# The first phase of a hybrid attention and convolution layer, rebuilt: latent tokens in two halves, adaLN in blocks of 256 channels by matmuls in four column strips

## The chip, the cores and the metric

One core of one Trainium2 chip runs the whole layer in one launch. The metric is the device time in microseconds (us), the median of the runs shown. The engines are named as in the profile: PE is the matrix engine (PEld its weight loads), DVE the vector engine, ACT the scalar engine, POOL the GpSimd engine. SP issues most of the DMAs. L12 is line 12 of the kernel. Lines of the kernel before are meant unless "of the changed kernel" stands beside them.

## The reference, cut to what matters

There are 1024 latent tokens and 256 context tokens of 1024 channels. All are normalised, scaled and shifted (adaLN), and go through one projection to 3840 columns that feeds three branches. The first phase of the kernel computes `h`.

```python
# D_MODEL = 1024, SEQ = 1024, CTX_LEN = 256, DEPTH = 1, all float32
def rmsnorm(x, g):
    y = x * lax.rsqrt(jnp.mean(x * x, axis=-1, keepdims=True) + NORM_EPS)
    return y * g
# per layer; the context goes through the same weights with c_ctx in place of c
shift, scale, gate = split3(silu(c) @ w_ada + b_ada)      # w_ada (1024, 3072)
h = rmsnorm(x, norm_g) * (1 + scale) + shift
z = h @ w_in                                              # w_in (1024, 3840)
# z: 4 x 256 columns short convolution, 4 x 512 attention (q, k, v, gate), 3 x 256 conformer
y = concat(short_conv_branch(...), neighbourhood_attention(...) * silu(gate), conformer_branch(...))
x = x + gate * (y @ w_out)
```

The attention's queries see a window of the latent grid, with a bias by relative position from a learned table, and all context keys.

## The kernel before

**Numbers in two parts.** For its large products PE takes each float32 array as a high and a low part (`hi`, `lo`), and three products replace one: high by high, high by low, low by high (`mm_k`, L374 to L376). So h is kept as `h0` (high) and `h1` (low), its context part as `hc0`, `hc1`, and the projection weights `wr` are split into `wh` by ACT (L128) and `wl` by POOL (L129).

**The first phase** is the function `start`. A string of tokens, `SEQ`, sets the order in which it emits its work, and on PE, DVE, ACT and POOL the work stays in that order. The DMAs all go through SP, one in-order queue, and eight semaphores in turn tell of their end, so each DMA there also waits for the one eight before it. The letters: `X` loads 128 tokens, `q` squares and sums them, `r` takes the inverse root, `x` scales them (L997). `L` loads adaLN weights. `a`, `b`, `c` transpose one block of 128 channels of the first latent half, the second latent half, or the context, so that channels lie on the partitions (`h_trans`, L327). `f`, `g`, `h` apply scale and shift and make the high part (`h_mod`); `u`, `v`, `o` make the low part (L351). `m`, `n` project a block of the first or second half onto the first pair's queries and keys. `Q` writes these to their tiles (queries L403, keys L422); `Q00` is followed by the scaling of the bias table `sg` (L498).

**adaLN** there is made per 128 channels, from rows of 512 bytes (L211), in three ways: blocks 0 and 6 by matmuls of split weights, blocks 1, 2 and 4 by float32 matmuls of two columns (`ada_mm32`, L241), blocks 3, 5 and 7 by products on DVE (`ada_acc`, L252 and L254), which small matmuls by ones then sum (L262). In h_mod, ACT (L342) or DVE (L340) writes the modulated block `h_raw` from PSUM, ACT copies its high part (L347), and DVE or POOL subtracts (L351).

**After the phase** PE's order is still the order of the code; the other engines and SP follow a scheduler's list. PE projects the context keys of the first pair (`proj_pair`), then the conformer's first two projections (`cf_in`: two of them, each over two latent halves, 24 matmuls per half), then the values (`v_proj`, L462). Beside that the bias tables are made: `sg` goes to the DRAM tables `dpr`, `dpm` (L503 to L509), from these to seven tables `u` (L517), from these to the tables `bt` of the first two heads (L533). The adaLN gate (`ada_gates`) loads 16 pieces `t` of weights (L840), and DVE sums them (L843, L845). The weights of the values are loaded at L448.

Of the kernel before, what the change touches and what calls it, by code (L numbers as in the profile page):

```python
# [52 lines left out]
g00 W00 C1 D301 b1 B2 g10 W10 v00 b3 w00 R2 b2 X1 v11 C2 w10 L40 X2 X0 X3 E3 n0 g21 g31 q10 v21 v31 q01 n1 n2 q20 L41  # L53
r02 L61 q30 L60 x11 r21 s61 x01 n3 s60 x21 L51 r31 x31 B4 a0 f01 t610 R4 a2 f21 u00 a1 t601 a3 W11 A6 D511 u20 f10 W01
m0 a4 u10 L50 C4 w01 f30 X9 b4 D501 m1 w11 f40 R6 L71 X8 u40 L70 u31 m2 C6 g40 a5 v40 q80 a6 E5 m3 q90 D701 f50 f60 n4
b6 D711 m4 b5 r82 u50 m5 g60 g50 v51 a7 b7 E7 x80 O x91 u60 f70 v60 g71 m6 n5 c0 u71 c1 h00 h11 m7 c3 c2 o01 Q00 n6
v70 o11 h20 n7 h31 o21 o31 Q02 Q01 Q10 Q12 Q11
# [3 lines left out]
def f32(ap):  # L61
    return ap.bitcast(F32)


class Builder:
# [14 lines left out]
    # ---- order of emission: TensorE work is traced in the order in which it shall run; coroutines  # L80
    # yield how far TensorE shall get before they go on ----
# [58 lines left out]
    def columns(self, name, rows):  # L140
        # rows of 128 channels, turned into one column per row
# [12 lines left out]
    def constants(self, crows):  # L154
# [8 lines left out]
        self.ones = cp.tile([P, 1], F32, name="ones")  # L163
        nc.gpsimd.memset(self.ones, 1.0)
# [6 lines left out]
        self.stat = stat = cp.tile([P, KT, 2, 2], F32R, name="stat")  # L171
        thv = th.rearrange("p (s k) -> p k s", s=2)
        self.stat32 = cp.tile([P, KT, 2], F32, name="stat32")
        nc.scalar.activation(out=self.stat32, in_=thv, func=AF.Copy, scale=0.5)
        nc.scalar.activation(out=stat[:, :, :, 0], in_=thv, func=AF.Copy, scale=0.5)
        self.stat_done = nc.vector.scalar_tensor_tensor(out=stat[:, :, :, 1], in0=thv, scalar=0.5, in1=f32(stat[:, :, :, 0]),
                                       op0=ALU.mult, op1=ALU.subtract)
# [28 lines left out]
    def ada_load(self, k, g):  # L206
        hk = KT // 2
        wa = self.sp_w.tile([P, hk, 2, P], F32, name="wa", bufs=7)
        for s in range(2):
            src = self.a["w_ada"][g * hk * P:(g + 1) * hk * P, s * D + k * P:s * D + (k + 1) * P]  # L210
# [3 lines left out]
    def ada_hi(self, w):  # L214
        hk = KT // 2
        wh = self.sp_w.tile([P, hk, 2 * P], F32R, name="wah", bufs=3)
        self.nc.scalar.activation(out=wh, in_=w, func=AF.Copy)
        return w, wh

    def ada_lo(self, w, wh, eng):  # L220
        wl = self.sp_w.tile([P, KT // 2, 2 * P], F32R, name="wal", bufs=3)
        eng.tensor_tensor(out=wl, in0=w, in1=f32(wh), op=ALU.subtract)
        return wh, wl

    def ada_mm(self, parts):
        nc = self.nc
        hk = KT // 2
        pa = self.ps_a.tile([P, HALF], F32, name="ps_a")
        for j in range(2):
            for kk in range(KT):  # L230
                st = self.stat[:, kk].rearrange("p s h -> p (s h)")
                nc.tensor.matmul(pa[0:4, 0:2 * P], lhsT=st, rhs=parts[kk // hk][j][:, kk % hk],
                                 start=(j + kk == 0), stop=(j == 1 and kk == KT - 1))
        return pa

    def ada_mm32(self, parts):
        nc = self.nc
        hk = KT // 2
        pa = self.ps_a.tile([P, HALF], F32, name="ps_a")
        for kk in range(KT):  # L240
            nc.tensor.matmul(pa[0:2, 0:2 * P], lhsT=self.stat32[:, kk], rhs=parts[kk // hk][:, kk % hk],  # L241
                             start=(kk == 0), stop=(kk == KT - 1))
        return pa

    def ada_acc(self, w, acc, g, first, eng):
        # half of the sum over 1024 rows for both conditioning vectors, still spread over the partitions
        hk = KT // 2
        for i in range(hk):
            for v in range(2):
                c, a = self.stat32[:, g * hk + i, v:v + 1], acc[:, v]  # L250
                if first and i == 0:
                    eng.tensor_scalar(out=a, in0=w[:, i], scalar1=c, scalar2=None, op0=ALU.mult)  # L252
                else:
                    eng.scalar_tensor_tensor(out=a, in0=w[:, i], scalar=c, in1=a, op0=ALU.mult, op1=ALU.add)  # L254

    def ada_sum(self, k, acc):
        nc = self.nc
        pa = self.ps_a.tile([P, HALF], F32, name="ps_a")
        for s in range(2):
            for v in range(2):  # L260
                c = 2 * s + v
                nc.tensor.matmul(pa[:, c:c + 1], lhsT=acc[:, v, s * P:(s + 1) * P], rhs=self.ones, start=True, stop=True)  # L262
        self.ada_mod(k, pa[:, 0:4].rearrange("p (s c) -> p s c", s=2))

    def ada_row(self, pa, n):
        row = self.sp_s.tile([4, 2 * P], F32, name="ada_row", bufs=1)[0:n]
        self.nc.scalar.activation(out=row, in_=pa[0:n, 0:2 * P], func=AF.Copy)
        return pa, row

    def ada_cols(self, k, pa, row):  # L270
        nc = self.nc
        n = row.shape[0]
        pt = pa[:, 2 * P:2 * P + 2 * n]
        for s in range(2):
# [958 lines left out]
```

## Time and profile before

| what | value |
|---|---|
| median of 3 runs (lowest to highest) | 637.64 us (636.84 to 638.3) |
| profiled execution, its span | 639.5 us |
| PE busy | 600.4 us, 94% of the span |
| DVE, ACT, POOL busy | 423.3, 258.0, 205.8 us |
| first phase on PE ends | 83.3 us |
| values' projection starts on PE | 109.70 us |
| granted PE clock 29.9 to 59.0 us, 59.0 to 83.3 us | 0.88, 0.86 |

The profiled execution has no time of its own but its span, 1.86 us above the median of the runs. The rows of the profile give the start in us, the duration, engine, line, operation, output and inputs, shapes and count; in brackets, how long the engine was idle before and what released it. A float32 matmul leaves two records. SPq is SP's queue as it issues DMAs.

### The profile page before, as it was taken

Reading aid. Unit: us, or ns where it says so; the run is one execution under the profiler, and the core shown is the slowest. Engines: PE = TensorE matmul, PEld = TensorE weight load, DVE = VectorE, ACT = ScalarE, POOL = GpSimd, SP = SyncE. Lnnn points to the kernel's source line nnn. Section 1 sums busy time; section 2 is a strip of 40 time slices with the busy share of each in tenths; the row PEclk is TensorE's granted clock in tenths of the full one; section 3 lists DMA queues with packets and bytes.
Section 4 is the critical chain, followed back from the end, with each engine's and each line's share of the span. In section 5 each row is a group of like instructions: output and inputs, shape, how many; then the busy total and the mean of one; then the engine's idle time right before and its main releaser. Section 6 shows DMA issues by size and latency. Waiting matters only on the chain.

```text
span 639.5 us, 9011 instructions
## 1 busy us (share of the span) xinstructions
PE 600.4 (94%) x3089; PEld 500.5 (78%) x3089; DVE 423.3 (66%) x709; ACT 258.0 (40%) x488; POOL 205.8 (32%) x213
## 2 busy tenths in 40 slices
PE   3888799969999999999999999999999999999995
PEld 1456678847889888888888888888887888888885
DVE  2889795848935669957889666773789726353343
ACT  4565571111125543344542455523645434331222
POOL 2467720021024322233331334232333261066112
PEclk9987899998999999999999999999999999999998
DMA  8991189454672303632116334145221165671122
GB/s 273 327 311 47 24 240 154 135 142 132 181 188 69 68 24 86 176 90 60 47 46 176 81 71 97 46 123 150 51 51 34 46 200 172 212 273 52 67 99 99
DMA packets 105619, 78.65 MB, mean 123 GB/s; under 512 B 26763, under 2 KB 89317, under 8 KB 105445
## 3 DMA queue, kind: packets, MB, share of 16 engines
q1 hardware_dynamic: 103845, 71.51, 41.2%
q10 hardware_dynamic: 1728, 6.55, 3.0%
q8 instruction: 25, 0.41, 0.3%
q14 instruction: 21, 0.17, 0.1%
HBM read 55.93 MB, written 14.29 MB: 110 GB/s over the span
## 4 chain that ended last, share of the span: by engine, by line
PE 73%; DVE 9%; SPq 5%; DMA 5%; issue 3%; POOL 2%; ACT 2%; POOLq 0%; DVEq 0%; ACTq 0%
PE ps_z L375 13%; PE ps_z L376 13%; PE ps_z L374 13%; PE po L651 5%; PE ps_t L639 5%; PE ps_f L898 5%; PE ps_f L900 5%; PE ps_f L899 5%; PE ps_s L620 3%; PE ps_s L621 2%; DVE acc L254 2%; PE ps_z L462 2%; SPq L211 2%; PE ps_z L464 2%; PE ps_z L463 2%
## 5 line engine op out<-in xcount | busy, mean ns | idle before, releaser
L374 PE MATMUL ps_z<-h,wh 128*128 128x512 f32 x408 | 162.0, 397 | 1.5 <-DVE kt L422 1.5
L375 PE MATMUL ps_z<-h,wh 128*128 128x512 f32 x408 | 160.8, 394 | 1.2 <-POOL h L351 1.2
L376 PE MATMUL ps_z<-h,wl 128*128 128x512 f32 x408 | 160.7, 394 | 0.0
L129 POOL TENSOR_TENSOR wl<-wr,wh 128x512 fp32r<-128x512 f32 x52 | 71.3, 1374 | 138.9 <-ACT wh L128 121.5
L630 POOL TENSOR_SCALAR pr<-pr,sm 128x640 f32<-128x640 f32 (+1 forms) x64 | 53.0, 828 | 138.5 <-DVE sm L629 122.7
L376 PEld LDWEIGHTS ps_z<-h,wl 128*128 128x128 f32 x408 | 77.3, 189 | 16.9
L374 PEld LDWEIGHTS ps_z<-h,wh 128*128 128x128 f32 x408 | 77.5, 190 | 14.9 <-issue 1.7
L375 PEld LDWEIGHTS ps_z<-h,wh 128*128 128x128 f32 x408 | 77.4, 190 | 14.6 <-POOL h L351 1.5
L716 DVE SCALAR_TENSOR_TENSOR acc<-t,half_w,acc 128x1024 f32<-128x1024 f32 x60 | 82.9, 1381 | 1.1
L643 ACT ACTIVATE pw<-ps_t 128x640 fp32r<-128x640 f32 (+1 forms) x64 | 43.5, 679 | 90.8 <-PE ps_t L639 90.8
L625 DVE CUSTOM_DVE_ANT_0 ps_s<-ps_s,bt 128x640 f32<-128x640 f32 (+1 forms) x64 | 50.9, 796 | 33.7 <-PE ps_s L621 31.9
L644 DVE TENSOR_TENSOR pw<-ps_t,pw 128x640 fp32r<-128x640 f32 (+1 forms) x64 | 50.4, 788 | 17.2 <-ACT pw L643 16.9
L628 ACT ACTIVATE pr<-ps_s,mn 128x640 f32<-128x640 f32 (+1 forms) x64 | 49.1, 766 | 20.0 <-DVE mn L625 19.2
L651 PE MATMUL po<-pw,vt 128*128 128x256 f32 x304 | 51.4, 298 | 2.1 <-DVE yb L602 1.2
L898 PE MATMUL ps_f<-woh,y 128*128 128x512 f32 (+1 forms) x136 | 51.6, 380 | 0.0
L900 PE MATMUL ps_f<-woh,y 128*128 128x512 f32 (+1 forms) x136 | 51.6, 379 | 0.0
L899 PE MATMUL ps_f<-wol,y 128*128 128x512 f32 (+1 forms) x136 | 51.6, 379 | 0.0
L128 ACT ACTIVATE wh<-wr 128x512 fp32r<-128x512 f32 x52 | 32.7, 628 | 38.3 <-PE ps_z L375 18.0
L639 PE MATMUL ps_t<-ident,pr 128*128 128x128 f32 x304 | 43.6, 272 | 0.0
L651 PEld LDWEIGHTS po<-pw,vt 128*128 128x128 f32 x304 | 40.4, 190 | 3.9 <-issue 3.5
L620 PE MATMUL ps_s<-kt,qd 128*128 128x384 f32 (+1 forms) x128 | 42.2, 350 | 0.5 <-ACT pr L628 0.4
L639 PEld LDWEIGHTS ps_t<-ident,pr 128*128 128x128 f32 x304 | 36.0, 142 | 1.7 <-issue 0.9
(174 smaller groups left out, 938.6 us busy)
## 6 DMA issues: line engine op xcount, KB each, us to landing
wr<-in_w_in SPq DMA_DIRECT2D x52, 256.0 KB
wa<-in_w_ada SPq DMA_DIRECT2D x32, 256.0 KB
qd<-qn SPq DMA_DIRECT2D x32, 256.0 KB
vd<-t SPq DMA_DIRECT2D x20, 256.0 KB
x_in<-in_x SPq DMA_DIRECT2D x8, 512.0 KB
t<-in_w_ada SPq DMA_DIRECT2D x16, 256.0 KB
vt<-vd SPq DMA_DIRECT2D x32, 128.0 KB
fraw<-in_w_out SPq DMA_DIRECT2D x8, 512.0 KB
```

What stands on the lines that cost most here:

```text
L129: i2 = (eng or nc.vector).tensor_tensor(out=lo, in0=src, in1=f32(hi), op=ALU.subtract)
L374: nc.tensor.matmul(ps, lhsT=wh, rhs=hh, start=(k == 0), stop=False)
L375: nc.tensor.matmul(ps, lhsT=wh, rhs=hl, start=False, stop=False)
L376: self.last = nc.tensor.matmul(ps, lhsT=wl, rhs=hh, start=False, stop=(k == KT - 1))
L620: nc.tensor.matmul(win, lhsT=q[:, b % 4], rhs=kwin, start=(i == 0), stop=(i == 1))
L630: nc.gpsimd.tensor_scalar(out=pr, in0=pr, scalar1=sm, scalar2=0.5, op0=ALU.mult, op1=ALU.mult)
L639: nc.tensor.transpose(out=pt[:, c * P:(c + 1) * P], in_=pr[:, c * P:(c + 1) * P], identity=self.ident)
L651: self.nc.tensor.matmul(po, lhsT=vt[:, vi, h], rhs=pw[:, c], start=(c == 0), stop=(c == n - 1))
L716: self.after_pe(nc.vector.scalar_tensor_tensor(out=acc, in0=u[:, t:t + T], scalar=self.half_w[:, 2 * t + ct:2 * t + ct + 1], in1=acc, op0= ...
L898: nc.tensor.matmul(ps, lhsT=yh, rhs=wh[:, ch], start=(first and i == 0), stop=False)
L899: nc.tensor.matmul(ps, lhsT=yh, rhs=wl[:, ch], start=False, stop=False)
L900: nc.tensor.matmul(ps, lhsT=yl, rhs=wh[:, ch], start=False, stop=(last and i == len(chs) - 1))
```

## The change

The first phase is rewritten; nothing behind the first context keys is, but for one swap on PE.

- The latent tokens go in two halves. Tokens 0 to 511 (`X0` to `X3`) are loaded first, and all of adaLN and of their projection (`a`, `f`, `u`, `m`) is done before tokens 512 to 1023 are squared and scaled; then come their `b`, `g`, `v`, `n`, then the context. Loads `X4` to `X9` stand last in the phase.
- adaLN is made per 256 channels in one way. `B(k, g)` issues four float32 matmuls, whose stationary operand is 32 columns (the two conditioning vectors, the rest zeros) and which stream 512 columns into the 32-partition strip i of one PSUM bank. `R` copies the bank to SBUF on ACT, `C` sums the strips by four small float32 matmuls with `sel` (ones where the strips have the two vectors), and three small DVE operations follow. The splits, the products on DVE and their sums by ones are gone.
- Its weights come in 16 loads of 512 KB in rows of 1 KB, where there were 32 loads of 256 KB.
- h_mod makes the high part on ACT straight from PSUM and the raw block on DVE, also from PSUM; the low part is always DVE's. All `x` scalings are on DVE.
- After the phase PE takes the first half of the first conformer projection ahead of the context keys.

```diff
 SEQ = """
-s00 X5 L10 K s01 t001 t010 A0 X7 X4 X6 L11 L31 q50 R0 q41 L20 C0 q70 L30 r42 x51 B1 q60 x41 r62 L21 D311 x70 x60 b0 R1
...
-v70 o11 h20 n7 h31 o21 o31 Q02 Q01 Q10 Q12 Q11
+X0 X1 L00 X2 X3 L01 K W00 W10 L10 L11 L20 L21 W01 W11 L30 L31 X4 X5 X6 X7 X8 X9
+q00 q11 r02 x01 x11 B00 q20 q31 r22 x21 x31 a0 a1 B01 R0 w00 w10 C0
+f0 u0 f1 u1
+B10 m0 B11 R1 m1 a2 C1 a3 f2 u2 f3 u3
+B20 m2 B21 R2 m3 w01 w11 a4 C2 a5 f4 u4 f5 u5
+B30 m4 B31 R3 q40 m5 q51 a6 C3 a7 f6 r42 u6 f7 u7 x41 x51 q60 q71 r62 x61 x71
+m6 m7 b0 b1 g0 v0 g1 v1 b2 O Q00
+n0 b3 g2 v2 n1 b4 g3 v3 n2 b5 g4 v4 n3 b6 g5 v5 n4 b7 g6 v6 q80 q91 n5 g7 v7 Q01 r82 n6 x81 x91 n7
+c0 Q02 c1 h0 o0 h1 o1 c2 c3 h2 o2 h3 o3 Q10 Q11 Q12
 """
...
     def ada_load(self, k, g):
         hk = KT // 2
-        wa = self.sp_w.tile([P, hk, 2, P], F32, name="wa", bufs=7)
+        wa = self.sp_w.tile([P, hk, 2, 2 * P], F32, name="wa", bufs=5)
...
+    def ada_mm(self, pa, w, g):
+
         hk = KT // 2
         for i in range(hk):
+            self.nc.tensor.matmul(pa[32 * i:32 * i + 32], lhsT=self.stat[:, g * hk + i], rhs=w[:, i],
+                                  start=(g == 0), stop=(g == 1))
+
+    def ada_row(self, pa):
+        row = self.sp_s.tile([P, HALF], F32, name="ada_row", bufs=1)
+        self.nc.scalar.activation(out=row, in_=pa, func=AF.Copy)
+        return row
 
     def ada_cols(self, k, pa, row):
         nc = self.nc
+        for i in range(4):
+            nc.tensor.matmul(pa[:, 2 * i:2 * i + 2], lhsT=row[:, i * P:(i + 1) * P], rhs=self.sel, start=True, stop=True)
...
+    def h_mod(self, ps, k, t0, src):
...
+        for i in range(1 + src):
+            scl, shift = self.scl[:, k + i, src:src + 1], self.shift[:, k + i, src:src + 1]
+            sl = slice(i * n, (i + 1) * n)
+            nc.scalar.activation(out=hi[:, sl], in_=ps[:, sl], func=AF.Identity, scale=scl, bias=shift)
+            nc.vector.tensor_scalar(out=raw[:, sl], in0=ps[:, sl], scalar1=scl, scalar2=shift, op0=ALU.mult, op1=ALU.add)
         return lo, raw, hi
...
-        self.run(self.proj_pair(0, self.ws[1]), self.cf_in(0))
+        first = self.cf_in(0)
+        self.run(itertools.islice(first, KT), self.proj_pair(0, self.ws[1]), first)
```

Three places in the order. On PE, the second block of 256 channels in the changed kernel (L223 is B, L322 to L324 a projection `m`, onto queries `ps_z_114` and keys `ps_z_115`, L278 transposes, L234 is C):

```order
L223 MATMUL ps_a<-wa,stat 32x512 x4
L322 MATMUL ps_z<-h_78,wh 128x512
L323 MATMUL ps_z<-h_79,wh 128x512
L324 MATMUL ps_z<-h_78,wl 128x512
L322 MATMUL ps_z<-h_78,wh 128x512
L323 MATMUL ps_z<-h_79,wh 128x512
L324 MATMUL ps_z<-h_78,wl 128x512
L278 MATMUL ps_h<-ident,x_in 128x128 x4
L234 MATMUL ps_a<-sel,ada_row 128x2 x4
```

Between B's second group and C of a block there now stand one projection and one transposed block, and no work of another half of the tokens.

On DVE, the end of the context's operands. The kernel before (`hc1` is the low part, `kt` and `qn` the writing of keys and queries, L843 the gate's first sums):

```order
L351 TENSOR_TENSOR hc1_92<-h_raw_762,hc0_91 128x512
L422 SCALAR_TENSOR_TENSOR kt_677<-ps_z_115,kt_677 64x512
L199 TENSOR_SCALAR half_w_789<-convc_787 128x62
L202 TENSOR_SCALAR half_ln_791<-convc_787 128x4
L422 SCALAR_TENSOR_TENSOR kt_677<-ps_z_115,kt_677 64x512
L403 TENSOR_TENSOR qn_676<-ps_z_116,qn_676 128x8x8x8
L422 SCALAR_TENSOR_TENSOR kt_677<-po_117,kt_677 64x512
L422 SCALAR_TENSOR_TENSOR kt_677<-ps_z_818,kt_677 64x256
L843 TENSOR_SCALAR acc_866<-t2_867,stat32_152 128x512
```

The changed kernel (L295 is the raw block, L299 the low part, L791 the gate's first sums):

```order
L299 TENSOR_TENSOR hc1_92<-h_raw_627,hc0_91 128x512
L295 TENSOR_SCALAR h_raw_633<-ps_h_622,scl_81,shift_80 128x256
L791 TENSOR_SCALAR acc_716<-t2_717,stat32_147 128x512
L295 TENSOR_SCALAR h_raw_633<-ps_h_622,scl_81,shift_80 128x256
L299 TENSOR_TENSOR hc1_92<-h_raw_633,hc0_91 128x512
L351 TENSOR_TENSOR qn_475<-ps_z_116,qn_475 128x8x8x8
L370 SCALAR_TENSOR_TENSOR kt_476<-po_117,kt_476 64x512
```

The gate's first sum now stands between the two raw halves of the last context pair, ahead of its low part; before, it stood behind the last low part and most of the keys.

On SP, the loads of the gate (`t2_…`) and of the bias tables. The kernel before:

```order
L509 DMA dpm_1057<-sg_678 312x1x16
L840 DMA t2_867<-in_w_ada 128x512
L840 DMA t2_876<-in_w_ada 128x512
L840 DMA t2_885<-in_w_ada 128x512
L840 DMA t2_894<-in_w_ada 128x512
L448 DMA t4_909<-in_w_in 128x2x512
L448 DMA yb_910<-in_w_in 128x2x512
L360 DMA wr_959<-in_w_in 128x4x128
L517 DMA u0_1072<-dpr_1058 312x8x8
```

The changed kernel, 23 `bt` loads and two `wr` loads after the last `u` (L465 is u, L481 bt, L788 the gate's, L396 the values'):

```order
L481 DMA bt0_953<-u6_951 32x1x64
L481 DMA bt1_957<-u0_939 24x1x64
L481 DMA bt1_957<-u0_939 72x1x128
L788 DMA t2_717<-in_w_ada 128x512
L788 DMA t2_726<-in_w_ada 128x512
L788 DMA t2_739<-in_w_ada 128x512
L788 DMA t2_754<-in_w_ada 128x512
L396 DMA acc_774<-in_w_in 128x2x512
```

The first gate load came right behind the five tables `dpr`, `dpm`; it now comes behind these, all seven `u` and 23 `bt` loads.

More of the change, by code (lines that the diff above doesn't have):

```diff
@@ L220, in ada_lo @@
[L220 to L245, printed above, removed]
+    def ada_mm(self, pa, w, g):
         hk = KT // 2
         for i in range(hk):
[L249 to L268, printed above, removed]
+            self.nc.tensor.matmul(pa[32 * i:32 * i + 32], lhsT=self.stat[:, g * hk + i], rhs=w[:, i],
+                                  start=(g == 0), stop=(g == 1))
@@ L270, in ada_cols @@
+    def ada_row(self, pa):
+        row = self.sp_s.tile([P, HALF], F32, name="ada_row", bufs=1)
+        self.nc.scalar.activation(out=row, in_=pa, func=AF.Copy)
+        return row
     def ada_cols(self, k, pa, row):
         nc = self.nc
-        n = row.shape[0]
-        pt = pa[:, 2 * P:2 * P + 2 * n]
-        for s in range(2):
-            nc.tensor.transpose(out=pt[:, n * s:n * s + n], in_=row[:, s * P:(s + 1) * P],
-                                identity=self.ident[0:n, 0:n])
-        if n == 2:
-            t = pt.rearrange("p (s c) -> p s c", s=2)
-        else:
-            t = self.sp_s.tile([P, 2, 2], F32, name="ada_t")
-            nc.vector.tensor_reduce(out=t, in_=pt.rearrange("p (s c h) -> p s c h", s=2, c=2), axis=AX.X, op=ALU.add)
@@ L291, in hsel @@
+        t = pa[:, 0:8].rearrange("p (s k c) -> p s k c", s=2, k=2)
+        ks = slice(2 * k, 2 * k + 2)
+        g, b, s = (self.mod[:, 8 * i:8 * i + 8][:, ks].unsqueeze(2).to_broadcast([P, 2, 2]) for i in range(3))
+        nc.vector.tensor_tensor(out=self.scl[:, ks], in0=t[:, 1], in1=s, op=ALU.add)
+        nc.vector.tensor_tensor(out=self.shift[:, ks], in0=t[:, 0], in1=b, op=ALU.add)
+        nc.vector.tensor_tensor(out=self.scl[:, ks], in0=self.scl[:, ks], in1=g, op=ALU.mult)
     def hsel(self, part, k, t0, n):
@@ L309, in square @@
         nc = self.nc
-        sq = f32(self.sp_w.tile([P, KT // 2, 2 * P], F32R, name="wal", bufs=3).rearrange("p k n -> p (k n)"))
+        sq = self.sp_h.tile([P, D], F32, name="sq", bufs=2)
         if eng is nc.scalar:
@@ L335, in h_mod @@
         n = HALF // (1 + src)
-        for i in range(1 + src):
-            scl, shift = self.scl[:, k + i, src:src + 1], self.shift[:, k + i, src:src + 1]
-            r, p = raw[:, i * n:(i + 1) * n], ps[:, i * n:(i + 1) * n]
-            if eng is nc.vector:
-                nc.vector.tensor_scalar(out=r, in0=p, scalar1=scl, scalar2=shift, op0=ALU.mult, op1=ALU.add)
-            else:
-                nc.scalar.activation(out=r, in_=p, func=AF.Identity, scale=scl, bias=shift)
         if src:
@@ L346, in h_mod @@
             hi, lo = self.hh(k, t0, n), self.hl(k, t0, n)
-        nc.scalar.activation(out=hi, in_=raw, func=AF.Copy)
+        for i in range(1 + src):
[3 more added lines that the diff above has]
+            nc.vector.tensor_scalar(out=raw[:, sl], in0=ps[:, sl], scalar1=scl, scalar2=shift, op0=ALU.mult, op1=ALU.add)
         return lo, raw, hi
@@ L957, in start @@
         crows = self.column_rows(self.c_parts())
-        was = {(0, g): self.ada_load(0, g) for g in range(2)}
         mrows = self.column_rows(self.mod_parts())
-        self.constants(crows)
         V, S, G = nc.vector, nc.scalar, nc.gpsimd
@@ L964, in start @@
         ss = self.sp_s.tile([P, 10], F32, name="ss", bufs=1)
-        parts, pa, pts, wr = {}, {}, {}, {}
+        was, pa, rows, pts, wr = {}, {}, {}, {}, {}
         self.ws = ws = [[None] * KT, [None] * KT]
+        self.constants(crows)
         def K():
@@ L981, in w @@
             ws[i][4 * g:4 * g + 4] = self.split_w(wr.pop((i, g)))
-        def s(k, g):
-            parts[k, g] = self.ada_hi(was.pop((k, g)))
-        def t(k, g, e=1):
-            parts[k, g] = self.ada_lo(*parts[k, g], (G, V)[e])
         def q(i, e):
@@ L999, in x, with B @@
                 S.activation(out=xs[i], in_=xs[i], func=AF.Copy, scale=ss[:, i:i + 1])
-        def A(k):
-            pa[k] = self.ada_mm([parts[k, g] for g in range(2)]), 4
-        def B(k):
-            pa[k] = self.ada_mm32([was.pop((k, g)) for g in range(2)]), 2
-        def da(k, g, e=1):
-            first = k not in parts
-            if first:
-                parts[k] = self.sp_w.tile([P, 2, 2 * P], F32, name="acc", bufs=2)
-            self.ada_acc(was.pop((k, g)), parts[k], g, first, (G, V)[e])
-        def E(k):
-            self.ada_sum(k, parts.pop(k))
+        def B(k, g):
+            if g == 0:
+                pa[k] = self.ps_a.tile([P, HALF], F32, name="ps_a")
+            self.ada_mm(pa[k], was.pop((k, g)), g)
         def R(k):
-            pa[k] = self.ada_row(*pa[k])
+            rows[k] = self.ada_row(pa[k])
         def C(k):
-            self.ada_cols(k, *pa.pop(k))
+            self.ada_cols(k, pa.pop(k), rows.pop(k))
         def ta(k):
```

52 lines of the change are left out of this document (18 added, 34 removed).

## The prediction

> **What bounds the kernel now.** I read the busy shares first (PE 94% of the 639.5 us span), then the windows, to find where PE is not full, then the timeline there, engine by engine.
>
> ```profile
> core 0: us, PE busy (x) PEld busy (x) DVE busy (x) ACT busy (x) POOL busy (x), PEclk, DMA share, GB/s
> 29.90:59.00 29.10, 23.96 (x121) 17.69 (x120) 26.16 (x39) 16.67 (x28) 17.89 (x14) 0.88 0.80 224
> 59.00:83.30 24.30, 20.75 (x97) 16.70 (x97) 19.83 (x34) 14.09 (x23) 16.62 (x18) 0.86 0.21 58
> 83.30:87.90 4.60, 3.12 (x27) 2.95 (x25) 4.25 (x7) 3.62 (x8) 2.53 (x2) 1.00 0.98 297
> 87.90:109.70 21.80, 21.80 (x96) 18.06 (x97) 14.18 (x19) 6.87 (x10) 1.91 (x3) 1.00 0.90 166
> 200.00:300.00 100.00, 99.80 (x570) 87.42 (x570) 72.24 (x131) 46.41 (x94) 30.57 (x31) 1.00 0.33 81
> 83.26 0.23 PE L145 MATMUL ps_a<-ident,rows 74*128 74x74 f32 x1
> 87.86 0.47 PE L374 MATMUL ps_z<-h,wh 128*128 128x512 f32 x1 [1.48 <-DVE kt L422]
> 109.70 0.40 PE L462 MATMUL ps_z<-wv,h 128*128 128x512 f32 x1
> ```
>
> PE is full from the conformer's projections on (21.80 of 21.80 us, then 99.80 of 100). So time is lost or won only before the values start, at 109.70. I forecast that start, T_v, and carry its shift to the end. The 96 matmuls of four half projections take 21.80, so a half takes 5.45 and a matmul .227; `m` or `n`, six of them, 1.36.
>
> **The change part by part.** Removed are DVE's products and the slow low parts on POOL, added is DVE and ACT work from PSUM:
>
> ```profile
> L254 DVE SCALAR_TENSOR_TENSOR acc<-wa,stat,acc 128x256 f32<-128x256 f32 x42 | 23.2, 619 | 0.3 <-DMA wa<-in_w_ada 0.3
> L351 POOL TENSOR_TENSOR h<-h_raw,h 128x512 fp32r<-128x512 f32 x10 | 20.8, 2092 | 13.1 <-ACT h L347 13.1
> L342 ACT ACTIVATE h_raw<-ps_h,shift,scl 128x512 f32<-128x512 f32 x11 | 8.5, 771 | 10.6 <-DVE scl L288 7.8 <-PE ps_h L327 1.4 <-POOL h L351 1.4
> 26.53 1.09 PE L327 MATMUL ps_h<-ident,x_in 128*128 128x128 f32 x8
> 29.73 0.21 DVE L286 TENSOR_SCALAR shift<-ps_a,modc 128x2 f32<-128x2 f32 x1
> 29.86 0.27 DVE L288 TENSOR_SCALAR scl<-ps_a,modc 128x2 f32<-128x2 f32 x1
> 30.45 1.52 DVE L340 TENSOR_SCALAR h_raw<-ps_h,scl,shift 128x512 f32<-128x512 f32 x2
> 31.95 1.41 DVE L351 TENSOR_TENSOR h<-h_raw,h 128x512 fp32r<-128x512 f32 x2
> 33.28 1.22 DVE L314 CUSTOM_DVE_ANT_0 wal<-x_in 128x1024 f32<-128x1024 f32 x1
> 35.59 3.62 PE L241 MATMUL ps_a<-wa,stat 128*2 128x256 f32 x16
> 35.67 1.42 DVE L997 TENSOR_SCALAR x_in<-x_in,ss 128x1024 f32<-128x1024 f32 x2 [1.16 <-POOL ss L320]
> 69.41 0.95 PE L262 MATMUL ps_a<-ones,acc 128*128 128x1 f32 x8
> 93.58 0.60 ACT L697 ACTIVATE t<-ps_z 128x512 f32<-128x512 f32 x1 [0.25 <-PE ps_z L376]
> 76.05 0.38 DVE L498 TENSOR_SCALAR sg<-sg 8x465 f32<-8x465 f32 x1
> GB/s 0 50 287 230 332 339 356 387 406 329 291 282 296 288 290 290 347 335 352 402 394 320 293 291 290 293 291 292 350 329 353 328 132 0 134 178 38 5 0 0
> ```
>
> Freed work buys nothing by itself: the question is how long the new chain of waits is. It has one unknown, B, PE's time for a group of four strip matmuls. Nothing before runs in strips. L241 shows 8 float32 matmuls of 256 columns in 3.62 us, .45 each, so .90 for 512 columns: four one after another take 3.6, four fully side by side .9. A float32 matmul leaves two records, of .45 here. If the two passes of one matmul follow each other in their strip, and only neighbouring matmuls overlap, four take 5 × .43 = 2.15. I take 2.15, between the ends, and keep both.
>
> The Trainium skill, "TensorE: Matmul & The Clock Gate", section "Part 3: Packing small matmuls — row/col tiling", gives 2.38× for three column strips of 512 columns, which speaks for the rival of strips side by side, below: four at the same share of the ideal would be an estimated B of 1.13 and 638.4 us by the sum. No run here shows strips.
>
> *First latent half.* `X0`, `X1`, `L00`, `X2`, `X3` are 3.15 MB; by the GB/s row (slices of 1.5 us) they have landed at 13.4. A square 1.22, the root's 1.16, two scalings 1.42: 17.2. Eight transposes 1.09: B's second group starts at 18.3. Behind B: R .60 (the ACT copy at 93.58), C .95 (eight records, as at 69.41), three small DVE operations .6, high part .77, raw .76, low part .70, and .5 for the hand-overs: 4.9. The first block is ready at 23.3 + B.
>
> Each further 256 channels has m 1.36, B, m 1.36 (R beside it), transposes .55, C .95, DVE .6, high .77, raw .76, low .70, hand-overs .35: 7.4 + B, since raw waits for ACT's read and nothing else fills PE. Three make 22.2 + 3B, the last block's pair another 1.46: 47.0 + 4B. The loads don't set this: 12.6 MB in all at 290 GB/s have landed by 51 (`X9`), and the context is needed near 66 + 4B.
>
> *Turn to the second half.* Two scalings 1.42, a square 1.22, root 1.25, two more scalings 1.42: 52.3 + 4B. Transposes .4, high .77, raw .76, `sg` .38, hand-overs .2: `sg` is ready at 54.8 + 4B. Before, it was ready at 76.43; with B = 2.15 it comes at 63.4, 13 us earlier.
>
> *Second half and context.* PE needs 1.91 per block (n and transposes), seven more blocks to 69.5 + 4B. The context pairs are set by ACT and DVE by turns:
>
> ```profile
> 77.39 1.00 DVE L340 TENSOR_SCALAR h_raw<-ps_h,scl,shift 128x256 f32<-128x256 f32 x2 [0.37 <-PE ps_h L327]
> 80.78 1.02 ACT L342 ACTIVATE h_raw<-ps_h,shift,scl 128x256 f32<-128x256 f32 x2 [1.24 <-POOL t L692]
> 76.46 0.29 SPq L503 DMA_DIRECT2D dpr<-sg  x1
> 77.85 0.85 SPq L509 DMA_DIRECT2D dpm<-sg  x1
> 78.75 1.96 SPq L840 DMA_DIRECT2D t<-in_w_ada  x4
> 84.99 0.84 SPq L517 DMA_DIRECT2D u<-dpr  x1
> 96.08 4.75 SPq L517 DMA_DIRECT2D u<-dpm  x3
> 112.55 1.32 SPq L840 DMA_DIRECT2D t<-in_w_ada  x3
> 122.35 9.75 SPq L533 DMA_DIRECT2D bt<-u  x13
> 115.61 1.42 DVE L845 SCALAR_TENSOR_TENSOR acc<-t,stat,acc 128x512 f32<-128x512 f32 x2 [2.61 <-DMA t<-in_w_ada]
> 89.64 0.88 DVE L843 TENSOR_SCALAR acc<-t,stat 128x512 f32<-128x512 f32 x2
> ```
>
> Per pair two high .51 and two raw .50, each raw behind its high, and the low .70 with hand-overs, 2.3; four pairs, the small constants 1.4 and waits at the turn 1.8 give the last low part at 81.9 + 4B, *if nothing else stands on DVE*.
>
> *The gate's first load.* But L791 of the changed kernel now stands there, and waits for `t2_717`, which SP issues behind the tables. From `sg` on SP spends 3.2 on the five `dpr` and `dpm` (.29 to .85 each, and their landing before the first `u`); seven `u`, four at .82 and three at 1.58, 8.0; 23 `bt` at .75 (9.75 for 13), 17.3; two `wr` .8: 29.3. From issue to use a load takes 3.06 (112.55 to 115.61). So `t2_717` is there 32.3 after `sg`, at 87.1 + 4B, later than DVE could come to L791 (about 80.5 + 4B). Then .45 for L791, raw .5, low .70: last low part at 88.8 + 4B. Queued behind L791 are that raw half and low part, which PE's context keys wait for, and the queries' and keys' sinks, for which the second conformer half waits (it takes over their PSUM bank). What the swap on PE puts ahead fills the hold with 5.45 us that no longer lie behind.
>
> The sum: PE has the last two context keys .8 behind the low part, then three half projections 16.35. T_v = 105.95 + 4B; with B = 2.15, 114.55 against 109.70: +4.85. The profiled span lies 1.86 above the median; the shift goes on the median: 637.64 + 4.85 = **642.5 us**. Edits at nothing: 1 KB rows (the loads end before they are needed; without that cover each 1% of 43 us of loading is .4 us), POOL's idle time (no one waits for POOL there), zero columns of the stationary (the load of weights stays beside the matmuls).
>
> **The rivals.**
>
> *Strips run one after another*, B = 3.6: +10.65, 648.3 us. For it: nothing of before overlaps float32 matmuls. Against: the outputs lie in different partitions of one bank.
>
> *Strips run fully side by side*, B = .9: T_v 109.55, −.15, 637.5 us: no change that can be told. (About .2%, 1.3 us, is what a measurement of this kernel can tell from none.)
>
> *The queue doesn't hold DVE.* If `t2_717` lands within 25.4 us of `sg`, the last low part is at 81.9 + 4B and T_v = 99.05 + 4B: with 2.15, 107.65, −2.05, 635.6 us. It decides by SP's time for 23 `bt`: at .45 each instead of .75 the hold of 6.9 is gone. For it: SP's .75 for `bt` come from a stretch in which the queue was full, and include waits for the semaphore of eight DMAs ago. Against: the `t` loads, at .49 each, show what a plain 256 KB issue costs, while `bt` moves small pieces. With strips side by side as well it comes to about −7, 630.6 us.
>
> *DVE shares with POOL.* The scalings that now all lie on DVE could be as slow as one of them was beside POOL's memsets:
>
> ```profile
> 70.72 4.69 DVE L997 TENSOR_SCALAR x_in<-x_in,ss 128x1024 f32<-128x1024 f32 x1
> 71.62 2.48 POOL L546 MEMSET bt<- 128x1408 f32 x2
> ```
>
> There one scaling took 4.69 instead of .71. In the changed chain two pairs of scalings and eight low parts are on the path; one such delay is +4 us, and would be added to each case. The `bt` memsets come after the phase's middle, on POOL as before, so I count half of one as a possible +2 in the range, not in the sum. A granted clock under .88 in the idle gaps would lengthen PE's .55 and 1.36 by an eighth, about 2 us over the chain, likewise. Neither has a chance of its own; they widen the other cases upwards.
>
> **How the numbers follow.** My forecast, hold and B near 2.15, has a chance of .38, with its own range 640 to 645.5; strips in a row .20; strips side by side with hold .20 (same .10, faster .07, slower .03); no hold .22 (faster .19, slower .03 where strips are in a row, which gives +3.75). Sums: faster .26, same .10, slower .64. The range leaves the far side-by-side-and-no-hold corner (630.6) and a delay on top of strips in a row out: 634.5 to 649.
>
> **What would show it.** The L223 group of the changed kernel: 2.15 us from the first start to the last end, against .9 or 3.6. First low part at 25.5, `sg` at 63.4. On DVE, before L791, an idle time of some 6 us ended by the DMA of `t2_717`; on SP, `bt` rows at .75 each before the first L788. Values' start at 114.5. The forecast is wrong if DVE shows no idle time there, if the values start before 108.4, or if PE has idle time again behind the values' start (the values' weights, loaded after the gate's pieces, are due near 104 + 4B).

## The result, and the profile after

The changed kernel takes 647.38 us in the median (645.08 to 648.59), the kernel before 637.97 in the median of the four runs beside it (636.84 to 640.82). The medians are 9.4 us apart; the ratio on record is 1.012, with a 95% interval of 1.0076 to 1.0164: about 7.6 us slower, and between 4.9 and 10.5. The profiled span went from 639.5 to 645.6 us, 6.1 more. The changed kernel's span of 645.6 belongs to a run of 647.4 us, 1.8 more; if that holds before too, the profile there is of an execution of some 641.3 us, longer than the four runs, and the spans understate the difference.

On PE, the rows of the changed kernel's timeline that answer to those of before (start, duration, engine, line, operation; in brackets the idle time ahead and what ended it):

```profile
20.26 1.93 PE L223 MATMUL ps_a<-wa,stat 128*32 128x512 f32 x8
36.74 1.07 PE L223 MATMUL ps_a<-wa,stat 128*32 128x512 f32 x8
105.97 0.58 PE L323 MATMUL ps_z<-hc,wh 128*128 128x256 f32 x1 [7.10 <-DVE hc L299]
124.63 0.40 PE L410 MATMUL ps_z<-wv,h 128*128 128x512 f32 x1
```

The values start at 124.63, 14.9 us later than before (109.70). 7.10 us of this is one wait for the last low part of the context. DVE's timeline shows why that part was late:

```profile
64.83 0.38 DVE L446 TENSOR_SCALAR sg<-sg 8x465 f32<-8x465 f32 x1
91.53 0.54 DVE L295 TENSOR_SCALAR h_raw<-ps_h,scl,shift 128x256 f32<-128x256 f32 x1
104.24 0.48 DVE L791 TENSOR_SCALAR acc<-t,stat 128x512 f32<-128x512 f32 x1 [12.17 <-DMA t<-in_w_ada]
104.65 0.54 DVE L295 TENSOR_SCALAR h_raw<-ps_h,scl,shift 128x256 f32<-128x256 f32 x1
105.22 0.69 DVE L299 TENSOR_TENSOR hc<-h_raw,hc 128x512 fp32r<-128x512 f32 x1
```

DVE stands 12.17 us at the gate's first sum, between the two raw halves of the last context pair. And SP, whose DMA it waits for:

```profile
65.24 0.29 SPq L451 DMA_DIRECT2D dpr<-sg  x1
...
67.72 2.47 SPq L465 DMA_DIRECT2D u<-dpr  x2
70.30 6.17 SPq L465 DMA_DIRECT2D u<-dpm  x3
76.51 4.63 SPq L465 DMA_DIRECT2D u<-dpr  x2
81.25 1.84 SPq L481 DMA_DIRECT2D bt<-u  x1
83.15 0.42 SPq L308 DMA_DIRECT2D wr<-in_w_in  x1
83.61 8.82 SPq L481 DMA_DIRECT2D bt<-u  x11
92.55 0.40 SPq L308 DMA_DIRECT2D wr<-in_w_in  x1
93.00 8.35 SPq L481 DMA_DIRECT2D bt<-u  x11
101.45 1.84 SPq L788 DMA_DIRECT2D t<-in_w_ada  x4
```

From the scaled bias table to the gate's first load SP is busy with tables for 36.2 us (65.24 to 101.45).

So far it is the hold of the prediction (DVE, and PE behind it, waiting for the gate's first load), only larger. But the values start 14.9 us later and the end comes only 6.1 later: 8.8 us are given back behind. In the kernel before, five rows that the prediction does not use, of PE, SP, ACT and DVE and of the windows:

```profile
143.73 0.77 PE L462 MATMUL ps_z<-wv,h 128*128 128x512 f32 x1 [5.87 <-DVE t L474]
133.57 1.28 SPq L360 DMA_DIRECT2D wr<-in_w_in  x2
137.34 0.63 ACT L128 ACTIVATE wh<-wr 128x512 fp32r<-128x512 f32 x1 [9.00 <-DMA wr<-in_w_in]
139.15 0.42 DVE L474 TENSOR_TENSOR t<-ps_z,t 128x256 fp32r<-128x256 f32 x1 [7.18 <-ACT t L473]
139.70:169.70 30.00, 25.97 (x104) 0.89 0.54 151
```

There PE stalls 5.87 us within the values' projection, and the granted clock in the 30 us from 139.7 is .89 (the last row, of the windows: PE busy 25.97, clock .89). ACT waits 9.00 for a weight whose load SP issued only at 133.57, behind the 13 `bt` loads in a row at 122.35. The changed kernel has issued 23 `bt` loads by then, and its PE has no wait there. The time from the values' start to the end of the span, the tail, is 529.8 us before (639.5 − 109.70) and 521.0 after (645.6 − 124.63). The whole difference lies in the values' projection: its 240 matmuls take 63.67 us before (109.70 to 173.37, where the next projection starts) and 54.86 after (124.63 to 179.49), 8.81 less. Of this 5.87 is the wait and about 2 the slow matmuls behind it (ten in 4.27 us, where ten at full speed take 2.33). About 1 is a pace of 5.60 us for 24 matmuls before, against 5.50 after, whose cause is not shown.

### The profile page after: what moved, and what is told of

It reads as the page before. It is cut to its first block, busy times and chain, and to the rows that moved or that the text cites. A ratio compares the mean times of both kernels' runs of the same rounds, so it can differ in the third digit from the quotient of the medians.

```text
span 645.6 us, 8868 instructions
## 1 busy us (share of the span) xinstructions
PE 596.8 (92%) x3071; PEld 495.1 (77%) x3071; DVE 410.0 (64%) x687; ACT 241.3 (37%) x463; POOL 176.7 (27%) x199
## 4 chain that ended last, share of the span: by engine, by line
PE 78%; DVE 4%; SPq 3%; ACT 2%; POOL 1%; issue 1%; DMA 0%; POOLq 0%; DVEq 0%; ACTq 0%
PE ps_z L322 13%; PE ps_z L323 13%; PE ps_z L324 13%; PE po L599 5%; PE ps_f L847 5%; PE ps_f L848 5%; PE ps_f L846 5%; PE ps_t L587 5%; PE ps_s L568 3%; PE ps_z L410 3%; PE ps_z L412 3%; PE ps_z L411 3%; SPq L481 3%; PE ps_s L569 2%; ACT pr L576 1%
## 5 line engine op out<-in xcount | busy, mean ns | idle before, releaser
L322 PE MATMUL ps_z<-h,wh 128*128 128x512 f32 x408 | 164.2, 402 | 1.5 <-ACT h L294 1.5
L324 PE MATMUL ps_z<-h,wl 128*128 128x512 f32 x408 | 161.4, 396 | 0.0
L322 PEld LDWEIGHTS ps_z<-h,wh 128*128 128x128 f32 x408 | 78.1, 191 | 21.5 <-ACT h L294 5.2
L324 PEld LDWEIGHTS ps_z<-h,wl 128*128 128x128 f32 x408 | 77.7, 190 | 17.3
L664 DVE SCALAR_TENSOR_TENSOR acc<-t,half_w,acc 128x1024 f32<-128x1024 f32 x60 | 80.8, 1347 | 1.1
L592 DVE TENSOR_TENSOR pw<-ps_t,pw 128x640 fp32r<-128x640 f32 (+1 forms) x64 | 50.4, 788 | 17.2 <-ACT pw L591 16.9
L131 ACT ACTIVATE wh<-wr 128x512 fp32r<-128x512 f32 x52 | 32.4, 628 | 31.8 <-PE ps_z L323 20.9
```

The costliest lines, as they stand in the source:

```text
L322: nc.tensor.matmul(ps, lhsT=wh, rhs=hh, start=(k == 0), stop=False)
L324: self.last = nc.tensor.matmul(ps, lhsT=wl, rhs=hh, start=False, stop=(k == KT - 1))
L664: self.after_pe(nc.vector.scalar_tensor_tensor(out=acc, in0=u[:, t:t + T], scalar=self.half_w[:, 2 * t + ct:2 * t + ct + 1], in1=acc, op0= ...
```

## The experiments

Tails are worked out as here, span less the values' start; stalls are PE's waits behind the values' start.

| kernel | ratio to before (95%) | values' start | stall behind | span | tail |
|---|---|---|---|---|---|
| before | 1 | 109.70 | 5.9 | 639.5 | 529.8 |
| changed | 1.012 (1.0076 to 1.0164) | 124.63 | none | 645.6 | 521.0 |
| gate's sum behind the sinks on DVE | 1.0119 (1.0092 to 1.0146) | 124.59 | none | 645.5 | 520.9 |
| tables behind the gate's loads on SP | 1.0118 (1.0092 to 1.0145) | 111.69 | 9.9 | 644.8 | 533.1 |
| before, tables spread | 0.9924 (0.9898 to 0.9951) | 110.15 | 3.0 | 634.9 | 524.8 |
| one strip | 658.91 us, one run | 135.79 | none | 656.7 | 520.9 |
| tables off SP | 1.0042 (1.0015 to 1.0069) | 110.68 | 4.9 | 638.1 | 527.4 |
| before, tables off SP | 0.9948 (0.9919 to 0.9977) | 107.95 | 4.5 | 637.6 | 529.7 |
| no swap | 1.0101 (1.0069 to 1.0132) | 124.53 | none | 645.2 | 520.7 |
| phase reordered, tables off SP | 0.9829 (0.9797 to 0.9861) | 102.42 | 4.1 | 628.7 | 526.3 |
| phase reordered alone | 0.9965 (0.9941 to 0.999) | 115.66 | none | 636.1 | 520.4 |
| the same with tables off SP and ACT reordered | 0.9775 (0.9745 to 0.9804) | 103.84 | none | 624.2 | 520.4 |

Tails without a stall are all 520.4 to 521.0, whatever stands in front. So what is between two profiled executions is in the start of the values, or in the stall and what comes with it. The tail isn't a fixed multiple of the stall: 5.9 us go with 8.8 more than the changed kernel's, and 4.5 with 8.7.

The starts themselves differ between executions. The changed kernel and those made from it (one strip aside) are alike up to their fifth group of strips, and that group starts at 36.74 in the changed kernel's profile, but elsewhere as early as 33.21 (tables behind). With the tables off SP, the first and the fifth group:

```profile
10.56 1.94 PE L223 MATMUL ps_a<-wa,stat 128*32 128x512 f32 x8 [6.88 <-DMA wa<-in_w_ada]
33.30 1.07 PE L223 MATMUL ps_a<-wa,stat 128*32 128x512 f32 x8
```

The first weights landed 2.0 us earlier there than in the changed kernel's profile (10.56 against 12.59), and PE came to full speed earlier (near 30 in place of 34). So among these kernels up to 3.5 us between two starts are not the edit's; the ratios of the times are the safer measure.

### Is it DVE's wait, or the late load?

```diff
                 self.after_pe(i)                    # the gate's sums
+                if k == 0:
+                    self.after(i, self.sink_last)   # behind the last latent sink on DVE
```

> The changed kernel, with one order added on DVE: the gate's first sum stays behind the last write of the first pair's latent keys, so that DVE does the last context low part and the sinks first. SP's order is as in the changed kernel. Theory (the gate's load, queued behind the tables, holds DVE and through it PE): the 7.1 us in which PE waits for the last low part and the slow clock behind it (1.7 us) are gone, the values start at 115.8 instead of 124.6, no stall comes back behind them, and the time falls by about 8.8 us to some 638.5, about the time of the kernel before. Rival (the values' weights, which come behind the gate's loads on SP and whose last load was issued at 111.7, end last): the values start or stall some 4 us later than that, and the time falls by only 4 to 5 us. Second rival (DVE's wait is covered by something else): no change.

DVE did the low part and the sinks at once, and the time did not move: 647.83 us. PE, ACT and SP:

```profile
109.67 0.79 PE L322 MATMUL ps_z<-h,wh 128*128 128x512 f32 x1 [7.42 <-ACT wh L131]
108.04 1.06 ACT L131 ACTIVATE wv<-t 128x1024 fp32r<-128x1024 f32 x1 [12.85 <-DMA t<-in_w_in]
101.84 0.38 SPq L398 DMA_DIRECT2D t<-in_w_in  x1
```

PE stands 7.42 us again, now at the conformer's projection. ACT's next work is the split of the values' weights, it waits 12.85 us for their load, and the split that PE needs stands behind. Both loads, the gate's and the values', come after the same tables on SP. My theory that DVE's place in the chain was the cause falls; the nearest rival named the right loads, but expected them to cost at the values and to leave a gain. What is left is the row on SP, with two engines that each have a waiting instruction at the front of their queues; the next run tests it.

### Is it the row on SP, and does it cost in both places?

```diff
+                    self.gate_dma = d               # the fourth load of the gate
...
                 d = dma(out=u.rearrange("q h r j -> (h r) q j"), in_=src)
+                self.after(d, self.gate_dma)        # all u, and so all bt, behind it
```

> The changed kernel, with one order added on SP: the seven u tables, and so all bt loads, stay behind the first four gate loads, as they stood in the kernel before. DVE's order is as in the changed kernel. Theory (two sides of one move: tables early on SP hold the gate, and late on SP hold the loads and stores of the values' stage): the hold of 7.1 us shrinks to about 1 us, since the gate's load then waits only for the last context transpose near 89.5, and the values start near 117; but the bt loads now stand before the stores of the values, and a stall of 6 us or more comes back behind the start of the values, with its slow clock, as in the kernel before: the time stays within 3 us of the changed kernel's. Rival (the stall of the kernel before, 5.9 us, had nothing to do with where the tables stand): no stall, and the time falls by 8 us.

```profile
PE ps_z L410 <- DVE t L422: 9.9, 2, 8.6
127.40 12.84 SPq L482 DMA_DIRECT2D bt<-u  x17
140.34 1.97 SPq L423 DMA_DIRECT2D vd<-t  x3
143.13 0.38 ACT L421 ACTIVATE t<-ps_z 128x256 fp32r<-128x256 f32 x1 [10.36 <-DMA vd<-t]
```

The first row is of the view of PE's waits (us in total, times, longest). The hold is gone, the values start at 111.69 (12.9 us earlier, of which 3.5 stand ahead of the fifth group), and 9.9 us of stall are back: 17 `bt` loads take 12.84 us of SP, the stores of the values (`vd`) stand behind them, and ACT waits 10.36 us for a tile that these free. The time is that of the changed kernel. This shows the two sides: early, the tables hold the gate's and the values' loads; late, the values' stores. Spreading them in the kernel before tests the late side alone:

```diff
-        for i in range(3):
-            self.bias_tables(0, i)
+        self.bias_tables(0, 0)
+        self.spawn(self.bias_late(), 6.0)           # the other 15 loads, 3 every 7 us of PE's work
```

> The kernel before, with 15 of its 21 bt loads of the first head spread over the projection of the values (three loads every 7 us of PE's work) in place of one row on SP. Theory: in the kernel before 13 bt loads in a row (9.75 us) keep the first stores of the values and the gate path's weights waiting on SP, ACT waits 9.0 us for these weights, DVE's low parts wait for ACT, and PE stalls 5.9 us at 143.7 with a slow clock behind it. Spread, the stall is gone and the time falls by 6 to 9 us, to 629 to 632. Rival (the stall comes from the tiles that the values are stored from, or from the stores' own landing): the stall stays, the time is the same within 1.5 us.

The stall fell from 5.9 to 3.0 and the time by .76% (635.42 against 640.28 us): the sign is the theory's, the size is less than its 6 to 9, and half of the stall stayed.

### What do the strips do?

```diff
-            self.nc.tensor.matmul(pa[32 * i:32 * i + 32], ..., start=(g == 0), stop=(g == 1))
+            self.nc.tensor.matmul(pa[0:32], ..., start=(g + i == 0), stop=(g == 1 and i == hk - 1))
```

> The changed kernel, with the four matmuls of each adaLN group all in the first strip, added up there, where the changed kernel has a strip for each; the copy and the sums then read 32 partitions. Theory (the strips run side by side): a group that took 1.06 at full clock takes 3.6 (four of .90), and one at the slow clock 1.93 becomes 6 or more; about four of them are on the chain, so the context operands end some 10 us later and the time rises by 8 to 12 us. Rival (the group is fast for another reason than the strips, the narrow stationary operand): it still takes about 1.06 and the time is the same.

The first and the second group of the phase in this kernel, on PE's timeline:

```profile
11.30 5.73 PE L223 MATMUL ps_a<-wa,stat 128*32 128x512 f32 x8 [7.41 <-DMA wa<-in_w_ada]
18.40 3.62 PE L223 MATMUL ps_a<-wa,stat 128*32 128x512 f32 x8
```

In one strip a group takes 3.62, in four 1.06 once PE runs fast. The first group, behind the wait for its weights, takes 5.73 against 1.94; at twice 3.62 it would be 7.2 if PE were slow throughout, so it seems to have sped up within. So the strips run side by side; the stationary operand has 32 columns in both, so its narrowness, the rival, isn't what makes a group fast.

The span grew by 11.1 us and the values' start by 11.2, but that isn't the strips' price, since the hold changed too:

```profile
77.00 16.48 SPq L481 DMA_DIRECT2D bt<-u  x20
111.41 1.79 SPq L788 DMA_DIRECT2D t<-in_w_ada  x4
```

SP issues 42 `bt` loads ahead of the gate's first load here (20, 11 and 11), in place of 23, and that load comes at 111.41 in place of 101.45. Ahead of the hold, DVE's last raw half ends 7.9 us later (99.93 against 92.07). How much the strips would cost without the hold is not shown.

### Does the swap on PE fill the hold?

```diff
-        self.run(itertools.islice(first, KT), self.proj_pair(0, self.ws[1]), first)
+        self.run(self.proj_pair(0, self.ws[1]), first)
```

> The changed kernel with PE's swap undone: the context keys come ahead of the conformer's first half projection again. In this order the gate's first sum stands behind the last low part and the first two sinks on DVE. The prediction's step, that the half projection put ahead fills 5.45 us of the hold: without it the time rises by about 5 us. Rival (the late loads hold whatever needs them next, and in this order PE has the context keys and the half projection before it meets the hold): PE does the same work before it stands still near 100 to 102, the stand still ends with the same loads, and the time is the same within 2 us.

The values start at 124.53 and the ratio is 1.0101 beside the changed kernel's 1.012: the time is the rival's. In this order the gate's sum stands further back on DVE too. PE stands still later, with all context keys and two half projections done, where the changed kernel had done one half and most of the keys:

```profile
112.08 0.77 PE L322 MATMUL ps_z<-h,wh 128*128 128x512 f32 x1 [3.98 <-DVE kt L370]
```

This wait ends at 112.08, not at 105.97: the write of the keys (`kt`) stands on DVE behind a split that needs ACT, and ACT waits 10.47 us for the values' weights. So late loads hold PE in this order too, as the rival has it, but not after the same work, and through another engine.

### What is left of the change when the tables are out of the way?

In both kernels the 21 `bt` loads of the first head were issued from ACT's queue, spread over the values' projection, those of the second head behind it; in the changed one the `u` tables stand behind the gate's first loads as above.

```diff
+                    dma = self.nc.sync.dma_start if only is None else self.nc.scalar.dma_start
...
+        self.spawn(self.bias_late(), 4.0)           # 3 loads every 5 us
```

> The changed kernel with the u tables behind the first four gate loads (as in the run with the tables behind), and besides the 21 bt loads of the first head issued from ACT's queue, three every 5 us of PE's work in the values' projection, and those of the second head on SP behind that projection. So neither the gate's load nor the values' stores have a row of table loads ahead of them. Theory (SP's one in-order queue, with some 30 us of table loads in it, is what costs the time wherever the row stands): no hold before the values (start at 112 to 116) and no stall behind; the 9.9 us of stall of the run with tables behind and its slow clock are gone, the span is near 632, the ratio to the kernel before .985 to .99. Rival (the values' stage has a stall of its own, from its tiles or from the stores of the gate, which come behind the u tables): 3 to 5 us of stall are left, ratio .99 to 1.00.

> The kernel before, with the same move of the table loads: 21 bt loads of the first head from ACT's queue, spread over the values' projection, the second head's on SP behind it. Theory: the stall behind the values' start, 5.9 us, of which 3.0 were left when 15 loads were spread on SP, is gone with its slow clock: 8.8 us less than the kernel before, ratio about .986. Rival (the 3.0 left are DVE's and ACT's own, the low part of a weight or the convolution's pieces between the values' low parts): the time of the spread run, ratio .992.

Each kept a stall of 4 to 5 us, so both rivals were nearer than the theory. Their ratio is 1.0042 / 0.9948 = 1.0094, some 6 us, near the 1.012 of the change as it was made. So the net loss is not the place of the tables, whose two sides nearly cancel. What is left of the change is the phase itself, and the swap on PE, which was tried only where the tables were early. In the profiled executions the values start 2.7 us later (110.68 against 107.95); where the rest of the 6 us lies is not shown: the first of these kernels ran between 639.87 and 646.32 us, the second between 632.72 and 639.43, and the profiled execution was near the low end of the one and at the high end of the other, so that their spans are only .5 us apart.

### Where is the phase's time?

With `SEQ` rewritten in its second half (squares and roots of the second half's tokens ahead of the last block's modulation, the context's squares and scalings on ACT within the second half, two context pairs among the last `n`), together with the tables off SP:

```diff
-B30 m4 B31 R3 q40 m5 q51 a6 C3 a7 f6 r42 u6 f7 u7 x41 x51 q60 q71 r62 x61 x71
+B30 m4 B31 R3 q40 m5 q51 q60 q71 r42 r62 a6 C3 a7 f6 u6 f7 u7 x41 x51 x61 x71
...
-n0 b3 g2 v2 n1 b4 g3 v3 n2 b5 g4 v4 n3 b6 g5 v5 n4 b7 g6 v6 q80 q91 n5 g7 v7 Q01 r82 n6 x81 x91 n7
-c0 Q02 c1 h0 o0 h1 o1 c2 c3 h2 o2 h3 o3 Q10 Q11 Q12
+n0 b3 g2 v2 q90 n1 b4 g3 v3 r82 n2 b5 g4 v4 x80 n3 b6 g5 v5 x90 n4 b7 g6 v6 n5 c0 g7 v7 n6 c1 h0 o0 n7
+Q01 h1 o1 c2 c3 h2 o2 Q02 h3 o3 Q10 Q11 Q12
```

> As the run with the tables off SP, and besides the hand-written order of the phase changed at its second half: the four squares and both roots of tokens 512 to 1023 go ahead of the last block's modulation, their four scalings right behind it; the context's squares and scalings go to ACT, within the second half; and two of the four context pairs are transposed among the last projections of the second half. Theory (the phase itself is a chain of waits, and of its PE idle time 2.7 us at the turn to the second half, 1.3 us at the first context transpose and most of the 3.3 us at the next two can be filled): the values start 5 us earlier than in the run with the tables off SP, and the time falls by another 4 to 6 us, ratio about .98. Rival (DVE, busy without gaps in the second half, sets its end): 1 to 2 us.

629.52 us, 13.9 less than with the tables off SP alone, where 4 to 6 were expected; in the profiled executions the values start 8.3 us earlier (102.42 against 110.68) and the spans are 9.4 apart. So the theory had the sign and less than half of the size; part of the 13.9 is that the profiled run with the tables off SP is an early one (639.91 us, where the median is 643.39). Then the same reordering with the tables left where the change has them:

> The changed kernel with only the reordering of the second half of the phase, and the tables where the changed kernel has them on SP. The bias table is then ready some 7 us earlier (57.6 where the changed kernel has 64.8), the context's operands some 8 to 10 us earlier. Theory (the hold ends with SP's row of tables, which starts at the bias table, so it moves with that and not with the phase's end): the gate's first load lands near 97, PE's wait for the last low part grows from 7 to about 10 us, the values start near 117, and the time falls by about 7 us, to the time of the kernel before. Rival (the phase's own end sets the time, the hold is covered): the values start near 105 and the time falls by 15 us or more.

```profile
94.06 0.49 DVE L791 TENSOR_SCALAR acc<-t,stat 128x512 f32<-128x512 f32 x1 [12.59 <-DMA t<-in_w_ada]
96.05 0.58 PE L323 MATMUL ps_z<-hc,wh 128*128 128x256 f32 x1 [8.75 <-DVE hc L299]
91.31 1.83 SPq L788 DMA_DIRECT2D t<-in_w_ada  x4
```

The hold moved with the bias table: `sg` at 57.21 in place of 64.83 (7.6 earlier, of which 3.0 stand ahead of the fifth group), the gate's first load issued at 91.31 in place of 101.45, behind 20 `bt` loads in place of 23, and PE's wait grew to 8.75. The values start at 115.66, 9 us earlier; the theory of the hold had 117. The ratio fell from 1.012 to .9965, some 10 us. So the end of the phase and SP's row are two limits side by side, and in the change as made SP's row ends last.

### The stall that was left

In the reordered kernel with the tables off SP, ACT's timeline around the first value tiles (L421 copies them, L131 splits weights, ACTq issues DMAs):

```profile
114.40 0.63 ACT L131 ACTIVATE wh<-wr 128x512 fp32r<-128x512 f32 x1 [0.17 <-DMA wr<-in_w_in]
114.42 2.84 ACTq L489 DMA_DIRECT2D bt<-u  x3
117.37 0.38 ACT L421 ACTIVATE t<-ps_z 128x256 fp32r<-128x256 f32 x1 [2.34 <-issue]
119.53 0.63 ACT L131 ACTIVATE wh<-wr 128x512 fp32r<-128x512 f32 x1 [1.77 <-DMA wr<-in_w_in]
121.67 0.63 ACT L131 ACTIVATE wh<-wr 128x512 fp32r<-128x512 f32 x1 [1.51 <-DMA wr<-in_w_in]
122.20 0.36 ACT L421 ACTIVATE t<-ps_z 128x256 fp32r<-128x256 f32 x1
```

Weight splits that wait for their loads, and the issue of three `bt` loads, stand ahead of the copies that free PE's PSUM banks.

```diff
         i1 = nc.scalar.activation(out=hi, in_=src, func=AF.Copy)
+        if self.evict is not None:
+            self.after(i1, self.evict)              # splits behind the copy of the fourth value tile
...
-        self.spawn(self.bias_late(), 4.0)
+        self.spawn(self.bias_late(), 9.0)
```

> As the run with the phase reordered and the tables off SP, and besides, on ACT, the splits of the gate path's weights behind the copies of the fourth value tile, and the first three bt loads 5 us later. Theory (the 4.1 us of stall that were left in the values' stage come from ACT's in-order work: it waits for four weight loads and issues three bt loads, 2.8 us, ahead of the copies of the first value tiles, for which PE's next PSUM bank waits): the stall and its slow clock are gone, 4 to 6 us less, ratio to the kernel before about .974. Rival (the copies are late because their tiles come free late, behind the stores of the gate): the stall stays within 1 us.

626.09 us, ratio 0.9775 (0.9745 to 0.9804): the stall is gone, the tail is 520.4 us, and this version beats both kernels, the one before by some 14 us. The two edits were made together, so which of them removed the stall is not shown.

## Why the prediction was right or wrong

**The direction, and the time (642.5; 647.38 measured, within the range of 634.5 to 649): right, but as a sum of two misses of opposite sign, and so in part by luck.** The values' start was put at 114.55, 4.85 later than before, and came 14.9 later; the shift was carried whole to the end, and 8.8 us of it came back. The two misses, 10.1 and 8.8, nearly cancel. What shows this is the tail in the table: 529.8 before, 521.0 after. The main case, with its own range of 640 to 645.5, is missed; and the case nearest to what came, strips side by side with the hold (.20), had 637.5 and no change.

**"I carry its shift to the end": the step that failed.** It rested on the window from 200 to 300 us and on the one up to 109.7. The window between them, which the prediction does not show, is not full:

```profile
109.60:200.00 90.40, 84.53 (x376) 69.14 (x375) 61.52 (x80) 19.25 (x43) 12.87 (x13) 0.96 0.55 148
```

PE is busy for 84.53 of its 90.40 us, and what is missing is the 5.87 us of the row at 143.73. And the stall's cause, `bt` loads in a row on SP, is the very row whose shift the prediction used against the gate: I asked what stands behind the tables where they now are, not what had stood behind them where they were.

**The hold: right in mechanism and place, too small.** It forecast some 6 us of idle time on DVE ended by the DMA of the gate's first load; 12.17 were measured. The mis-sized terms: SP's seven `u` tables, 8.0 forecast from their issues, took 13.4 (67.72 to 81.14), with waits; 23 `bt` loads 17.3 forecast, 19.0 measured (1.84 + 8.82 + 8.35); together 36.2 us from `sg` to the load in place of 29.3. The issue-to-use time was right (3.06 forecast, 2.79 measured).

**"Queued behind L791 are that raw half and low part": true, and not the point.** With L791 taken out of the way nothing was gained, since ACT has the next late load at the front of its queue. The hold came from SP's row; DVE's place in it could be taken by ACT.

**B, the strips.** I took 2.15 and gave .9 as one end. Side by side was right: 1.06 at full speed. But the first four groups ran at 1.93 to 1.94, two of them on the chain, so the four groups there cost about 6.0 (1.93 + 1.94 + 1.06 + 1.06) for the forecast 8.6. Put into the prediction's sum, that gives a values' start of 111.95. The Trainium skill, "TensorE: Matmul & The Clock Gate", section "Part 3: Packing small matmuls — row/col tiling", which gives 2.38× for three column strips, points the same way: here four strips give 3.62 / 1.06 = 3.4×.

**The chain of the phase.** `sg` was forecast at 63.4 and came at 64.83. So with 2.6 us less for the strips, the other terms were 4 us too short: the second group started at 20.26 in place of 18.3, since the second pair of tokens landed late (its square began at 15.12, behind a wait of 4.51 us for the load that was counted as landed at 13.4) and its scaling ended at 18.94 in place of 17.2. And the first `C` took 1.87 in place of .95 at slow speed. Most of the 4 us belongs to the execution and not to the chain: with the tables off SP, where the first weights landed 2.0 us earlier, `sg` came at 61.24. Without the hold I had forecast the values' start at 107.65, 2 us earlier than before. With the hold removed it was 111.69 and 110.68, both in executions some 3.5 us ahead of the changed kernel's at the fifth group. That the change is slower by some 6 us with the tables dealt with alike is the part of the result that I had with the wrong sign.

**DVE beside POOL.** The delay that was allowed in the range, and not in the sum, is there: a low part took 1.55 us in place of .69 (at 74.42, with a weight split on POOL from 74.13 to 75.42), and two scalings 2.42 in place of 1.42 (at 80.76, with another split from 81.37 to 82.64). Whether they set the phase's end is not shown.

**The swap: wrong.** "What the swap on PE puts ahead fills the hold with 5.45 us" presumes a hold at a fixed place in PE's order. Without the swap the time is the same.

**The edits at nothing** (1 KB rows, POOL, zero columns): none was tried apart, and nothing in the runs speaks for or against them alone.

## What to carry to other kernels

A long row of small DMAs on an in-order queue cost time here wherever it stood; ask what is queued behind it in the old place as well as in the new, and spread it or give it another queue rather than move it. Before a shift is carried to the end, read PE's waits up to the end; a wait that is already there can go when the work behind it moves. And if a wait is removed on one engine, look for the next instruction, on any engine, that waits for the same late data.

## What the runs showed of the hardware

Four column strips of float32 matmuls with 512 columns ran 3.4 times as fast as the same four in one strip (1.06 against 3.62 us, both at PE's full speed).

PE ran slow where the granted clock doesn't tell it. In the windows view of the changed kernel (PE's busy time and matmuls, granted clock, DMA share, GB/s):

```profile
12.00:24.00 12.00, 7.32 (x30) 1.00 1.05 322
105.90:109.60 3.70, 3.63 (x11) 0.52 0.97 339
```

The group at 20.26 took 1.93 us in a window with a clock of 1.00; the matmuls behind the 7.10 us wait took .63 in place of .40 for some 3.7 us, and there the clock shows .52. The Trainium skill, "TensorE: Matmul & The Clock Gate", section "Part 1: The HAM clock gate", puts the return to full speed after about 3.4 us of sustained work; the second case agrees with 3.7, and the first, where PE had gaps, ran slow up to 34 us.

One `bt` load costs SP .80 us (8.82 for 11), though it moves 6 to 36 KB, and a 256 KB load of the gate's weights .46 (1.84 for four).
